# Row vectors written to DRAM four values at a time, and read back through strided views

## The chip, the cores and the metric

One core of a Trainium2 chip runs the whole program in one launch. The metric is the device time of one execution in microseconds (us). TensorE does the matrix products, VectorE (DVE in the profile) and GpSimd (POOL) the elementwise work, ScalarE (ACT) the activations and copies, and SyncE (SP) issues every DMA, strictly in the order of its queue.

## The reference

Two blocks run one after the other on one sequence of 512 tokens with 1024 features, in float32. The first block has two layers (a gated MLP mixer, then a sparse attention mixer, each followed by a squared-ReLU feed-forward of width 4096); the second is one layer of two attentions. Cut to what matters here:

```python
def modulate(h, shift, scale):
    return h * (1.0 + scale[:, None, :]) + shift[:, None, :]
...
    for layer in range(DEPTH):
        mod = c_act @ ada_w[layer] + ada_b[layer]
        sh1, sc1, g1, sh2, sc2, g2 = jnp.split(mod, 6, axis=-1)
        h = modulate(rms_norm(x, norm_g[layer, 0]), sh1, sc1)
        ...
        x = x + g1[:, None, :] * rms_norm(y, norm_g[layer, 1])
        h = modulate(rms_norm(x, norm_g[layer, 2]), sh2, sc2)
        y = jnp.square(jax.nn.relu(h @ ff_w_in[layer])) @ ff_w_out[layer]
        x = x + g2[:, None, :] * rms_norm(y, norm_g[layer, 3])
    return x
```

Each shift, scale and gate is a vector of 1024 values, one for each feature, and the same for all tokens. The second block ends with `x + gate * out` and has such a vector too.

## The kernel before

**Tiles.** Tokens are cut in four chunks of 128 (c0 to c3). The running sum `x` has its tokens on the partitions, one tile of 128x1024 for each chunk. The products take their operand with the features on the partitions, so at each boundary between two stages a chunk of `x` is normalised, scaled, shifted, transposed on TensorE and split in a high and a low half.

**Row vectors.** `vec` and `mod` compute a vector on VectorE (products of the transposed weights with the condition `cb`, 1 MB of weights at a time). It then lies on 128 partitions with 8 values in each: value 128k + p is in partition p, column k. `col` finishes it. Where the vector must multiply tiles with tokens on the partitions, it is needed as a row, the same on all partitions, and `wide` makes this: SP writes the 128x8 values to a scratch tensor of 1024 values in DRAM, and reads it back twice, each time 512 values copied to all 128 partitions. Eleven vectors go this way: G1, B2, S2 (end of the first mixer), G2 (end of the first feed-forward), G3, B4, S4 (end of the sparse attention), G5, B6, S6 (end of the second feed-forward), and the last gate. In the profile a copy has the vector's name with a w: G1w.

**Boundaries.** When a chunk's output product is done (its accumulator is `acc`, two banks of 512 columns), `residual` squares it on ScalarE, multiplies it by G on VectorE (`z<-acc,G1w`, two instructions of 512 columns), and adds it, scaled, to `x`. `x_rstd` makes the norm on ScalarE (`junkx`) with some small instructions. `h_chunk` multiplies by B (`hx<-x,B2w`, twice) and adds S (`hx<-hx,xr,S2w`, twice), then TensorE transposes (`tp<-ident,hx`). At the end of the first feed-forward `h_chunk2` does this with columns in place of rows, so that only the two products with G2 read a row there. In `fin`, the end of the program, the output is multiplied by the gate (`fy<-acc,gatew`), added to `x` and stored; the last 512 columns of c3 go in two halves.

**Order.** A planner (`Rec`) puts every instruction in a fixed order on each engine, by modelled costs and due times that come from the shapes. Each engine works in that order, and so does SP's DMA queue: a transfer that waits holds up all that stand behind it. In `out_gemm`, the products of the last `tail` weight rows run chunk after chunk, and the transposes of a chunk stand among the products of the next one, at the place where the planner expects their operand.

Of the kernel before, what the change touches and what calls it, by code (L numbers as in the profile page):

```python
# [672 lines left out]
class KB:  # L673
# [279 lines left out]
    def wide(self, vec, name):  # L953

        v = self.col(vec)
        r = self.scratch([1, 1024], name)
        self.sp.dma_start(r.rearrange("o (k p) -> p (o k)", p=128), v)
        t = [self.t2([128, 512], F32, name) for _ in range(2)]
        for n in range(2):
            self.sp.dma_start(t[n], r[:, n * 512:n * 512 + 512].bcast())  # L960
        return t


    def x_rstd(self, c, either=False):
# [32 lines left out]
    def h_chunk(self, c, r, B, S, hT, keep=None):  # L997
        if keep is not None:
            return self.h_chunk2(c, r, B, S, hT, keep)
        for n in range(2):  # L1000
            s = slice(n * 512, n * 512 + 512)
            t = self.t2([128, 512], F32, "hx")
            self.flex("tensor_mul", t, self.xs[c][:, s], B[n])
            self.mac(t, t, r, S[n])
            ps = self.ps("tp")
            for j in range(4):
                self.pe.transpose(ps[:, j * 128:(j + 1) * 128], t[:, j * 128:(j + 1) * 128], self.ident)
            cs = slice(c * 128, c * 128 + 128)
            self.split(hT.hi[n][:, :, cs], hT.lo[n][:, :, cs], ps.rearrange("p (j t) -> p j t", j=4))
# [17 lines left out]
    def residual(self, c, banks, G):  # L1027

        ss = self.st(2, "ys")
        z = []  # L1030
        for n in range(2):
            s = slice(n * 512, n * 512 + 512)
            junk = self.t2([128, 512], F32, "junk")
            self.act.activation(junk, banks[n], AF.Square, accum_out=ss[:, n:n + 1])
            z.append(self.t2([128, 512], F32, "z"))
            self.dve.tensor_mul(z[n], banks[n], G[n])
        r = self.rstd_of(ss, "yr")
        for n in range(2):
            s = slice(n * 512, n * 512 + 512)
            x = self.xs[c][:, s]  # L1040
            self.mac(x, z[n], r, x)
# [638 lines left out]
    def second(self, hT, grow):  # L1680
# [298 lines left out]
        gate = self.wide(grow, "gatew")  # L1979

        def fin(c, banks):
            for n in range(2):
                s = slice(n * 512, n * 512 + 512)
                xt = self.t2([128, 512], F32, "fx")
                self.sp.dma_start(xt, self.xd[c][:, s])
                y = self.t2([128, 512], F32, "fy")
                parts = 2 if c == NC - 1 and n == 1 else 1
                for i in range(parts):
                    h = slice(i * 512 // parts, (i + 1) * 512 // parts)
                    self.dve.tensor_mul(y[:, h], banks[n][:, h], gate[n][:, h])  # L1990
                    self.dve.tensor_add(y[:, h], y[:, h], xt[:, h])
                    self.sp.dma_start(self.out[0, c * 128:(c + 1) * 128, n * 512 + h.start:n * 512 + h.stop], y[:, h])

        self.out_gemm(self.act_f32(mixed), I["w_out_2"][0], KD, fin, CTAIL, split=True)

    def build(self):
# [87 lines left out]
```

## Time and profile before

| | |
|---|---|
| time before, median of 3 runs | 1547.93 us (1546.73 to 1547.94) |
| the profiled execution's own time | 1551.01 us |
| span of the profile | 1549.2 us |
| TensorE products busy | 1497.3 us, 97% |
| VectorE busy | 1084.5 us, 70% |
| ScalarE, GpSimd busy | 660.7 us, 284.8 us |
| chain that ended last, by engine | PE 83%, DVE 9%, DMA 3%, ACT 2%, issue 2%, POOL 1% |
| mean granted clock of TensorE | 0.989 |

The profile is one execution. Busy time is summed for each engine over the whole span; the chain that ended last is followed back from the last instruction, at each step to what it had waited for. All instructions that the planner emits have one line of the program (L616), so that the tiles' names tell them apart. Times in the trace count from the start of the span.

### The profile page before, as it was taken

The page shows a single profiled execution, that of the slowest core. Times are in us where ns is not written, and L with a number is a line of the kernel's source. Part 1 is how long each engine was busy: PE and PEld are TensorE (multiplying, and loading weights), DVE is VectorE, ACT ScalarE, POOL GpSimd, SP SyncE. Part 2 cuts the span into 40 slices and gives each one's busy share as a digit, 9 for nine tenths or more (in the row PEclk, how much of TensorE's full clock was granted, in tenths as well). Part 3 has the DMA queues.
Part 4 walks back from the last instruction along what each step waited for, and adds up shares of the span by engine and source line. Part 5 has one row for each costly group of instructions (what it writes and reads, how often), then busy time and mean ns, then how long its engine had stood idle before and what let it go on. Part 6 is the DMA issues. An engine that isn't in the chain of part 4 may idle for free.

```text
span 1549.2 us, 20191 instructions
## 1 busy us (share of the span) xinstructions
PE 1497.3 (97%) x7426; PEld 1253.7 (81%) x7426; DVE 1084.5 (70%) x2035; ACT 660.7 (43%) x1430; POOL 284.8 (18%) x349
## 2 busy tenths in 40 slices
PE   8995899999999999999998999999999999999998
PEld 6884688888888889788877898888888888878877
DVE  8895685557874378778898674556663568788992
ACT  6531342232121455577786332222120337667780
POOL 1122000000010130265655000000000004123250
PEclk9998899999999999999999999999999999999999
DMA  9872289447931071300015356538412161113212
GB/s 369 270 265 53 84 259 333 149 162 282 357 123 41 28 255 55 114 1 28 28 29 179 103 168 204 174 99 250 183 55 68 55 222 52 58 41 101 50 55 95
DMA packets 126370, 212.97 MB, mean 137 GB/s; under 512 B 24512, under 2 KB 85184, under 8 KB 126272
## 3 DMA queue, kind: packets, MB, share of 16 engines
q1 hardware_dynamic: 126272, 211.69, 41.0%
q8 instruction: 58, 0.95, 0.3%
q14 instruction: 40, 0.33, 0.1%
HBM read 205.33 MB, written 6.34 MB: 137 GB/s over the span
## 4 chain that ended last, share of the span: by engine, by line
PE 83%; DVE 9%; DMA 3%; ACT 2%; issue 2%; POOL 1%; POOLq 0%; SPq 0%; DVEq 0%; ACTq 0%
PE acc L616 28%; PE fmps L616 27%; PE vps L616 4%; PE qps L616 4%; PE tmc L616 4%; PE po L616 3%; DVE wl L616 2%; PE sgps L616 1%; PE tmb L616 1%; PE kps L616 1%; PE sB L616 1%; PE sA L616 1%; PE tp L616 1%; DVE ptl L616 1%; DMA G1w<-G 1%
## 5 line engine op out<-in xcount | busy, mean ns | idle before, releaser
L616 DVE TENSOR_TENSOR wl<-raw,wh 128x1024 fp32r<-128x1024 f32 x194 | 243.7, 1258 | 38.7 <-PE fmps L616 18.5
L616 PE MATMUL acc<-wl,ah 128*128 128x512 f32 x432 | 168.6, 390 | 0.0
L616 PE MATMUL acc<-wh,ah 128*128 128x512 f32 x432 | 168.4, 390 | 0.0
L616 DVE CAST wh<-raw 128x1024 fp32r<-128x1024 f32 x114 | 80.5, 706 | 120.6 <-PE fmps L616 94.4
L616 DVE SCALAR_TENSOR_TENSOR raw<-raw,cb 128x1024 f32<-128x1024 f32 x112 | 136.1, 1241 | 8.0 <-DMA raw<-in_kv_ada_w_dram 7.9
L616 PE MATMUL acc<-wh,al 128*128 128x512 f32 x432 | 133.6, 390 | 0.0
L616 ACT ACTIVATE r<-fmps 128x512 f32<-128x512 f32 x64 | 38.2, 597 | 205.9 <-PE fmps L616 205.9
L616 PE MATMUL acc<-twh,tah 128*128 128x512 f32 x272 | 106.9, 401 | 18.5 <-DVE twh L616 18.5
L616 PE MATMUL acc<-twl,tah 128*128 128x512 f32 x272 | 106.1, 399 | 0.5 <-DVE twl L616 0.5
L616 PE MATMUL fmps<-hfh,wl 128*128 128x512 f32 (+1 forms) x288 | 105.3, 367 | 0.7 <-DVE wl L616 0.7
L616 PE MATMUL fmps<-hf1l,wh 128*128 128x512 f32 (+1 forms) x288 | 105.4, 366 | 0.0
L616 PE MATMUL fmps<-hfl,wh 128*128 128x512 f32 (+1 forms) x288 | 105.4, 366 | 0.0
L616 PE MATMUL fmps<-hf1h,wl 128*128 128x512 f32 (+1 forms) x288 | 105.4, 366 | 0.0
L616 PE MATMUL fmps<-hfh,wh 128*128 128x512 f32 (+1 forms) x288 | 105.1, 366 | 0.0
L616 PE MATMUL fmps<-hf1h,wh 128*128 128x512 f32 (+1 forms) x288 | 105.0, 366 | 0.0
L616 ACT CAST ah<-hid 128x512 fp32r<-128x512 f32 x48 | 29.8, 620 | 158.9 <-PE acc L616 158.9
L616 PEld LDWEIGHTS acc<-wl,ah 128*128 128x128 f32 x432 | 81.2, 188 | 16.7
L616 PEld LDWEIGHTS acc<-wh,ah 128*128 128x128 f32 x432 | 81.1, 188 | 16.7
L616 PEld LDWEIGHTS acc<-wh,al 128*128 128x128 f32 x432 | 81.1, 188 | 16.7
L616 POOL TENSOR_SCALAR tah<-hid 128x512 fp32r<-128x512 f32 x4 | 4.2, 1038 | 471.6 <-DMA raw<-in_ff_w_out_dram 206.2
L616 PE MATMUL acc<-twh,tal 128*128 128x512 f32 x272 | 88.1, 398 | 0.6 <-DVE tal L616 0.6
L616 ACT CAST wh<-raw 128x1024 fp32r<-128x1024 f32 x59 | 61.8, 1050 | 50.5 <-PE fmps L616 35.5
(528 smaller groups left out, 3847.5 us busy)
## 6 DMA issues: line engine op xcount, KB each, us to landing
raw<-in_ada_w_dram SPq DMA_DIRECT2D x40, 1024.0 KB, 7.2
raw<-in_ff_w_in_dram SPq DMA_DIRECT2D x32, 1024.0 KB, 9.1
raw<-in_ff_w_out_dram SPq DMA_DIRECT2D x32, 1024.0 KB, 5.3
raw<-in_w_in_dram SPq DMA_DIRECT2D x16, 1024.0 KB, 5.5
raw<-in_w_ada_dram SPq DMA_DIRECT2D x12, 1024.0 KB, 11.5
raw<-in_ada_w_dram SPq DMA_DIRECT2D x16, 512.0 KB, 9.7
raw<-in_kv_ada_w_dram SPq DMA_DIRECT2D x8, 1024.0 KB, 14.3
raw<-in_a_w_in_dram SPq DMA_DIRECT2D x8, 512.0 KB, 10.2
```

Source lines behind the costliest of these rows:

```text
L616: getattr(real[e], m)(*a, **k)
```

## The change

`wide` writes the vector to DRAM in another order. In each half of 512 values, the four values that a partition has of this half now lie side by side: value 128k + p of a half goes to place 4p + k. What a partition writes is two runs of 4 values (16 bytes) in place of eight single values (4 bytes). The two reads that copy a half to all partitions are as before, so the copies have this order too, and `wide` gives out views of them with two free dimensions, k (step 1) and p (step 4), which run through the values in the old order. The instructions that read a row take these views; their other operands are viewed with the same two dimensions by `by4`, in which the values still lie side by side.

```diff
@@ wide
         v = self.col(vec)
         r = self.scratch([1, 1024], name)
-        self.sp.dma_start(r.rearrange("o (k p) -> p (o k)", p=128), v)
+        self.sp.dma_start(r.rearrange("o (n p k) -> p (o n) k", n=2, p=128), v.rearrange("p (n k) -> p n k", n=2))
         t = [self.t2([128, 512], F32, name) for _ in range(2)]
         for n in range(2):
             self.sp.dma_start(t[n], r[:, n * 512:n * 512 + 512].bcast())
-        return t
+        return [x.rearrange("q (p k) -> q k p", k=4) for x in t]
+
+    @staticmethod
+    def by4(x):
+
+        return x.rearrange("q (k p) -> q k p", k=4)
@@ h_chunk
-            self.flex("tensor_mul", t, self.xs[c][:, s], B[n])
-            self.mac(t, t, r, S[n])
+            self.flex("tensor_mul", self.by4(t), self.by4(self.xs[c][:, s]), B[n])
+            self.mac(self.by4(t), self.by4(t), r, S[n])
@@ residual
-            self.dve.tensor_mul(z[n], banks[n], G[n])
+            self.dve.tensor_mul(self.by4(z[n]), self.by4(banks[n]), G[n])
@@ fin
-                    self.dve.tensor_mul(y[:, h], banks[n][:, h], gate[n][:, h])
+                    hk = slice(h.start // 128, h.stop // 128)
+                    self.dve.tensor_mul(self.by4(y)[:, hk], self.by4(banks[n])[:, hk], gate[n][:, hk])
```

## Rows read from the trace of the kernel before

**Rows 1.** The chain of waits, 120 to 180 us: start, duration, what.
```profile
127.41 9.87 DMA B2w<-B
...
138.20 11.71 DMA G1w<-G
...
150.38 7.04 DMA raw<-in_a_w_out_dram
...
161.18 11.09 DMA S2w<-S
...
172.34 3.71 DMA S2w<-S2w
```
**Rows 2.** Timeline of PE, 118 to 210 us; in brackets its idle time before.
```profile
158.35 1.19 PE L616 MATMUL acc<-twh,tah 128*128 128x512 f32 x2 [18.46 <-DVE twh L616]
...
177.05 0.63 PE L616 MATMUL tp<-ident,hx 128*128 128x128 f32 x4 [1.97 <-DVE hx L616]
```
**Rows 3.** Windows: from:to, length, busy of PE to POOL, PEclk, DMA share, GB/s.
```profile
128.00:129.00 1.00, 0.96 (x4) 0.83 (x5) 1.00 (x1) 0.01 (x1) 0.00 (x0) 1.00 0.47 4
129.00:130.00 1.00, 1.00 (x7) 0.79 (x6) 1.00 (x4) 0.00 (x0) 0.00 (x0) 1.00 0.00 0
...
142.00:143.00 1.00, 0.00 (x0) 0.00 (x0) 0.00 (x0) 0.00 (x0) 0.00 (x0) 1.00 0.00 0
...
144.00:149.00 5.00, 0.00 (x0) 0.00 (x0) 0.00 (x0) 0.00 (x0) 0.00 (x0) 0.50 0.00 0
...
158.40:162.00 3.60, 3.60 (x9) 2.83 (x10) 2.75 (x4) 0.16 (x1) 0.00 (x0) 0.50 0.00 0
```
**Rows 4.** DMA issues of the run: size of one, median us to landing.
```profile
out_dram<-fy SPq DMA_DIRECT2D x2, 128.0 KB, 1.8
```
**Rows 5.** Groups of VectorE instructions by form: count, busy us, mean ns, idle before.
```profile
L616 DVE SCALAR_TENSOR_TENSOR bl<-R,pos,bh 128x124 fp32r<-128x124 f32 x32 | 13.2, 427 | 1.0 <-ACT bh L616 0.8
...
L616 DVE SCALAR_TENSOR_TENSOR mx<-pm,lngb,E 128x512 f32<-128x512 f32 x8 | 5.9, 744 | 1.5 <-PE pm L616 1.5
...
L616 DVE TENSOR_TENSOR z<-acc,G3w 128x512 f32<-128x512 f32 x8 | 5.2, 685 | 11.6 <-PE acc L616 11.6
...
L616 DVE SCALAR_TENSOR_TENSOR E<-wsum,lngb,bs 128x128 f32<-128x128 f32 x8 | 2.3, 336 | 0.0
```
**Rows 6.** Timeline of VectorE at the end of the first mixer, 164 to 178 us.
```profile
164.89 1.29 DVE L616 TENSOR_TENSOR z<-acc,G1w 128x512 f32<-128x512 f32 x2 [3.74 <-PE acc L616]
...
168.52 0.22 DVE L616 SCALAR_TENSOR_TENSOR rt<-yr,hv 128x1 f32<-128x1 f32 x1 [0.87 <-ACT yr L616]
...
176.15 1.41 DVE L616 SCALAR_TENSOR_TENSOR hx<-hx,xr,S2w 128x512 f32<-128x512 f32 x2 [3.19 <-DMA S2w<-S2w]
```
**Rows 7.** Timeline of VectorE at the end of the second feed-forward, chunk c0.
```profile
1208.60 1.29 DVE L616 TENSOR_TENSOR z<-acc,G5w 128x512 f32<-128x512 f32 x2 [31.22 <-PE acc L616]
...
1212.49 1.29 DVE L616 TENSOR_TENSOR hx<-x,B6w 128x512 f32<-128x512 f32 x2
1213.80 0.15 DVE L616 TENSOR_SCALAR hv<-ss 128x1 f32<-128x1 f32 x1
...
1214.90 1.42 DVE L616 SCALAR_TENSOR_TENSOR hx<-hx,xr,S6w 128x512 f32<-128x512 f32 x2
```
**Rows 8.** Timeline of PE there: the transposes of c0.
```profile
1216.56 0.60 PE L616 MATMUL tp<-ident,hx 128*128 128x128 f32 x4
```
**Rows 9.** Windows (columns as in rows 3): ends of the attention and the second feed-forward.
```profile
860.00:903.00 43.00, 43.00 (x252) 37.81 (x252) 36.68 (x77) 17.28 (x48) 1.67 (x1) 1.00 0.51 176
1208.00:1258.00 50.00, 50.00 (x238) 41.51 (x237) 36.90 (x84) 20.88 (x52) 3.26 (x4) 1.00 0.49 168
```
**Rows 10.** Timeline of VectorE and PE at the end of the first feed-forward, chunk c0.
```profile
522.72 0.48 DVE L616 TENSOR_SCALAR hx<-x,xr 128x512 f32<-128x512 f32 x1
...
524.15 1.03 PE L616 MATMUL tp<-ident,hx 128*128 128x128 f32 x8
```
**Rows 11.** Timeline of VectorE at the end of the program.
```profile
1545.02 0.76 DVE L616 TENSOR_TENSOR fy<-acc,gatew 128x256 f32<-128x256 f32 x2 [1.30 <-PE acc L616]
```

## The prediction

> **What bounds the kernel now.** I read the page first: TensorE is busy 97% of the span, so nearly every microsecond in which it stands still is on the path, and work on other engines counts only where TensorE waits for it. The chain of waits, in order of time, then shows where DMAs end last: the row vectors appear on it in one place only, the end of the first mixer [rows 1]. SP stands there behind the write of B2 (9.87 us), then behind that of G1 (11.71 us), and the load of the last rows of the mixer's output weights can only be issued after both, at 150.38. The timeline of PE shows what this costs: 18.46 us of standstill before 158.35 [rows 2]. S2's write (11.09 us) and its read back (3.71 us) are on the chain next; VectorE waits 3.19 us for them [rows 6] and TensorE 1.97 us [rows 2]. At the ends of the attention and of the second feed-forward TensorE is busy in all of the 43 and 50 us [rows 9], though VectorE makes every chunk's operand there.
>
> **What the write of a vector is made of.** In windows of 1 us, B2's write moves its packets between 128 and 129 (DMA share 0.47); from 129 on nothing moves, and yet it lands only at 137.28 [rows 1, 3]. So about 1.6 us pass to the last packet and 8.3 us after it, while 1024 single values settle in DRAM. I take the second part to go with the number of runs, 256 in place of 1024: 8.3/4 + 1.6 = 3.7 us. Bounds: 1.8 us, the landing of a store of 128 KB in long runs [rows 4], and no change. The nearer is the low one, since the settling is all of the difference to that store. G1's write shares the DMA engines with B2's two reads; its packets are through by 142 [rows 3], and of its 11.71 us the last 7.9 shrink to 2.0, leaving 5.8. S2's becomes 1.6 + 9.5/4 = 4.0 us.
>
> **What this gives at the first mixer's end.** G1's write is issued 0.92 us after B2's has landed, and the weight load 0.47 us after G1's [rows 1]. The load goes out at 127.41 + 3.7 + 0.92 + 5.8 + 0.47 = 138.3, 12.1 us earlier, and TensorE resumes at 158.35 - 12.1 = 146.3. It still stands for over 6 us. TensorE's clock fell to the lower of its two levels (granted 0.50) by 144, some 4 us into the standstill, and was still there after the restart [rows 3]; I assume that it falls again, so nothing is given back for it. With the 1.97 us wait gone, the transposes of c0 could run at 177.05 - 1.97 - 12.1 = 163.0. VectorE decides: its first product with G1 moves from 164.89 to 152.8; from there to the end of its first `hx<-hx,xr,S2w` (176.15 + 0.75) it took 12.0 us, of which the 3.19 for S2 go, because S2 is back at 161.18 - 12.1 + 4.0 + 3.7 = 156.8, before its turn. That would be 161.6 without dearer reads.
>
> **What a strided read costs.** 89 instructions read a row with step 4: 32 with G, 24 with B (one on GpSimd), 24 with S, 9 with the gate. The trace has no such step, but one neighbour: `bl<-R,pos,bh` reads one of its inputs with a step of 16 values and takes 427 ns for 124 columns [rows 5]. The same operation without the step takes 336 ns for 128 columns (E) and 744 for 512 (mx), which makes 1.06 ns a column and 200 ns fixed, so 332 ns for 124. The step costs 95 ns in 124 columns, 0.77 ns each, and 0.40 us in 512. The view in three dimensions alone costs nothing: mx has one too, and lies on the line of its kind. Bounds for 512 columns: nothing (a step of four values is nearer to contiguous than one of 16), and 0.54 us, a second pass over the 512 columns at 1.06 ns. I take 0.40, from the row. [...]
>
> **Where it falls on the path.** In c0 of the first mixer, seven such instructions come before the first transposes (four z, two of them c1's, two B, one S): 2.8 us, of which some 0.6 disappear in a wait for ScalarE (0.87) [rows 6]. c0's transposes then run at 161.6 + 2.8 - 0.6 + 0.1 = 163.9, against 177.05: **13.1 us gained**. From c1 to c3 VectorE is nearly saturated and the transposes stand in TensorE's queue just behind their operand; six instructions add 2.4 us a chunk, less some 0.4 of slack: 3 x 2.0 = **6.0 us lost** (c3 has one fewer on VectorE, but no slack).
>
> The other ends have the same pattern with nothing to win. At the end of the second feed-forward c0's chain runs z (two), x, B (two), small instructions, S (two). `hv` follows B with no gap [rows 7], so all six are in line. The first S ends at 1215.65, the transposes begin at 1216.56 [rows 7, 8]: 0.9 us of slack, 0.75 after the hand-over. TensorE takes the transposes in order, among c1's products, so it stands 2.4 - 0.75 = 1.65 us, the next chunk's accumulator is late by as much, and the same happens again. There are four chunks here and four at the end of the attention: 8 x 1.65 = **13.2 us lost**. At the end of the first feed-forward only the two z are slower, 0.8 us against about 0.9 of slack between the normalised chunk and its transposes [rows 10]: nothing, and what is over 0.75 if the step is dearer. At the end of the program two products of 256 columns stand in a row before the last store [rows 11]: **0.4 us**. The write costs of the other eight vectors lie under products of TensorE and give nothing back. The planner's costs come from shapes that don't change, so I expect the same order.
>
> **Sum.** 13.1 - 6.0 - 13.2 - 0.4 = -6.5: slower by 6.5 us. The profiled execution took 1551.01 us, 3.08 above the median of the runs; 1557.5 for it, and 1547.93 + 6.5 = 1554.4, so 1554 us, for the median. With the step at 0.30 or 0.50 us and all else alike, the sum runs from 1 us faster to 13 slower: 1547 to 1561 is this case's own range.
>
> **Rivals.**
> *The strided reads are (nearly) free.* Place: the eight chunks above. Below some 0.12 us an instruction the slack of 0.75 swallows them, and only the first mixer's gain is left. For it: no row has a step as short as four values. Against: the row with 16. At no cost TensorE sets c0's transposes at 163.0, 14 us gained: 1534 us; at 0.2 us, 1540. The point where it turns is near 0.3. [...]
> *A strided column takes a whole second pass* (0.54 us). For it: the row lies at three quarters of that. 12.1 - 8.5 - 8 x 2.49 - 0.5 = -17: 1565 us, and the queues fill further beyond. [...]
> *The write does not get shorter.* Then nothing is gained at the first mixer, its c0 hides its dearer reads in the 3.19 us wait, and 6.0 + 13.2 + 0.4 make 1567 us. For it: the DMA engines are idle for most of the write, so the packets' number is not what they work on. Against: the settling is absent for long runs [rows 4].
> *The clock stays up*, because the write lands in 2 us and the standstill ends before 144. TensorE's products up to c0's end then run at the full level, which is worth at most half of the 6.5 us from 158.35 to 164.89; I take 2.6, with 2 more from the writes: 1550 us, and 1546 with the step at 0.35 us.
>
> **Chances.** The forecast 0.54; free reads 0.18; second pass 0.13; write unchanged 0.07; clock up 0.08. A measurement here can tell some 0.2% (3.1 us) from no change. Faster by more: nearly all of the free reads, half of the clock case and a little of the first, 0.22. Within: a third of the forecast and most of the rest of the clock case, 0.20. Slower: 0.58. For 8 in 10 the range takes in the unchanged write and half of the two stride rivals: 1538 to 1570.
>
> **What would show it.** In the profile after: writes of vectors landing in 3 to 6 us, SP issuing the weight load near 138, TensorE's standstill at 6 us; `z`, `hx` and `fy` with rows at 1.05 to 1.15 us in place of 0.68 to 0.75; short waits of TensorE for `hx` in each of the eight chunks of rows 9's stretches, 1 to 2 us each. The forecast is wrong if those instructions keep their time, if TensorE stays busy in those stretches in spite of them, or if the writes still take 10 us.

## The result, and the profile after

| | before | after |
|---|---|---|
| median of the runs on one chip | 1547.93 us (1546.73 to 1548.36) | 1558.3 us (1554.39 to 1559.49) |
| ratio, with its 95% interval | | 1.0057 [1.0041, 1.0072] |
| the profiled execution's own time | 1551.01 us | 1554.39 us |
| span of the profile, mean granted clock | 1549.2 us, 0.989 | 1552.6 us, 0.993 |
| TensorE, VectorE busy | 1497.3, 1084.5 us | 1501.0, 1117.3 us |
| DMA packets, of them under 512 bytes | 126370, 24512 | 117922, 16064 |
| chain that ended last | PE 83%, DVE 9%, DMA 3% | PE 77%, DVE 15%, DMA 1% |

The change makes the kernel slower, by 10.4 us in the medians and by 3.4 us in the two profiles (why these differ is taken up with the last experiment). Every engine runs the same instructions on the same tiles in the same order as before, so the traces can be compared row by row. The chain already points the way: DMA's share of it falls from 3 to 1%, and VectorE's rises from 9 to 15%.

The gain is where it was expected, at the end of the first mixer. The chain of waits there, in the columns of [rows 1]:

```profile
127.36 2.56 DMA B2w<-B
...
130.85 3.19 DMA G1w<-G
...
134.50 7.44 DMA raw<-in_a_w_out_dram
```

The two writes take little over a quarter of their time [rows 1], and the weight load goes out 15.9 us earlier. The timeline of PE:

```profile
142.88 0.70 PE L616 MATMUL acc<-twh,tah 128*128 128x512 f32 x2 [2.99 <-DVE twh L616]
...
159.34 0.63 PE L616 MATMUL tp<-ident,hx 128*128 128x128 f32 x4 [0.73 <-DVE hx L616]
...
168.15 0.63 PE L616 MATMUL tp<-ident,hx 128*128 128x128 f32 x4 [1.66 <-DVE hx L616]
```

The standstill is 2.99 us in place of 18.46, and c0's transposes come 17.7 us earlier [rows 2]; but TensorE now waits for `hx` in all four chunks: 0.73 and 1.66 us in the lines above, 1.22 us in c2 (at 178.11) and 2.06 us in c3 (192.44), where before it waited 1.97 us in c0 and 1.05 us in c3. Of the other writes, four in the list of DMA issues (size, us to landing; before, these four took 11.1, 11.0, 9.9 and 9.7 us):

```profile
S2w<-S SPq DMA_DIRECT2D x1, 4.0 KB, 1.6
...
G2w<-G SPq DMA_DIRECT2D x1, 4.0 KB, 2.9
...
G3w<-G SPq DMA_DIRECT2D x1, 4.0 KB, 1.7
...
G5w<-G SPq DMA_DIRECT2D x1, 4.0 KB, 3.0
```

The slowest of the rest are S4's, 16.8 us before and 2.7 after, and S6's, 13.5 and 6.1.

What takes the gain back stands in the groups of VectorE by form, here two of before,

```profile
L616 DVE SCALAR_TENSOR_TENSOR hx<-hx,xr,S6w 128x512 f32<-128x512 f32 x8 | 5.7, 748 | 0.1
...
L616 DVE TENSOR_TENSOR hx<-x,B6w 128x512 f32<-128x512 f32 x8 | 5.1, 686 | 0.0
```

and four of after:

```profile
L616 DVE SCALAR_TENSOR_TENSOR bl<-R,pos,bh 128x124 fp32r<-128x124 f32 x32 | 13.2, 426 | 1.0 <-ACT bh L616 0.8
...
L616 DVE SCALAR_TENSOR_TENSOR hx<-hx,xr,S6w 128x512 f32<-128x512 f32 x8 | 8.7, 1131 | 0.1
...
L616 DVE TENSOR_TENSOR hx<-x,B6w 128x512 f32<-128x512 f32 x8 | 8.3, 1082 | 0.0
L616 DVE TENSOR_TENSOR z<-acc,G3w 128x512 f32<-128x512 f32 x8 | 8.3, 1067 | 11.0 <-PE acc L616 11.0
```

The `z` with G3 took 685 ns [rows 5] and now takes 1067; the `hx` with B6 and with S6 took 686 and 748 ns and now take 1082 and 1131. That is 0.38 to 0.40 us for 512 columns, or 0.75 to 0.77 ns a column. With B2, B4 and the gate it is 0.37 to 0.41 us, with S4 0.49 in the mean, where one pair of instructions took 2.96 us (at 881.32) and the others 2.18 to 2.24. `bl`, which the change doesn't touch, is as it was. The windows that answer to [rows 9], and two of the low clock (columns as in [rows 3]):

```profile
144.00:148.00 4.00, 3.93 (x11) 2.77 (x10) 1.68 (x3) 0.00 (x0) 0.00 (x0) 0.58 0.04 1
...
860.00:903.00 43.00, 37.83 (x231) 33.27 (x231) 41.49 (x67) 14.86 (x39) 1.98 (x1) 0.96 0.64 217
884.00:888.00 4.00, 3.58 (x17) 3.51 (x18) 4.00 (x7) 1.60 (x5) 0.00 (x0) 0.58 1.08 381
1208.00:1258.00 50.00, 44.67 (x207) 35.55 (x206) 41.48 (x71) 17.57 (x43) 2.85 (x4) 1.00 0.51 169
```

TensorE, which filled both stretches [rows 9], now stands for 5.17 of 43 and 5.33 of 50 us. In the first of them the waits for `hx` over 0.3 us are 0.95, 1.35, 1.31 and 0.97 us (c0, c1 and the two halves of c2; c3 has none). In the second stretch the timeline of PE names who was late, in each of the four chunks:

```profile
1213.94 0.63 PE L616 MATMUL tp<-ident,hx 128*128 128x128 f32 x4 [0.88 <-DVE hx L616]
...
1227.21 0.63 PE L616 MATMUL tp<-ident,hx 128*128 128x128 f32 x4 [0.91 <-DVE hx L616]
...
1242.21 0.63 PE L616 MATMUL tp<-ident,hx 128*128 128x128 f32 x4 [1.74 <-DVE hx L616]
...
1256.70 0.63 PE L616 MATMUL tp<-ident,hx 128*128 128x128 f32 x4 [1.00 <-DVE hx L616]
```

**A table by stage.** SP issues the write of a vector at a fixed place in the kernel's order, so these writes cut the span in five stretches. In the timeline of SP, first before, then after:

```profile
223.30 0.37 SPq L616 DMA_DIRECT2D G2w<-G  x1
...
795.77 0.38 SPq L616 DMA_DIRECT2D G3w<-G  x1
...
925.27 0.37 SPq L616 DMA_DIRECT2D G5w<-G  x1
...
1453.05 0.37 SPq L616 DMA_DIRECT2D gatew<-gate  x1
```

```profile
209.65 0.37 SPq L616 DMA_DIRECT2D G2w<-G  x1
...
782.58 0.38 SPq L616 DMA_DIRECT2D G3w<-G  x1
...
921.61 0.37 SPq L616 DMA_DIRECT2D G5w<-G  x1
...
1456.07 0.37 SPq L616 DMA_DIRECT2D gatew<-gate  x1
```

The first stretch holds the end of the first mixer, the third the end of the attention, the fourth that of the second feed-forward. So the first stretch became 13.7 us shorter, the second 0.5 longer, the third 9.5, the fourth 6.7 and the last 0.4. The experiments are read by these stretches.

### The profile page after: what moved, and what is told of

The parts are those of the page before. It is cut to its first block, busy times and chain, and to the rows that moved or that the text cites. A ratio compares the mean times of both kernels' runs of the same rounds, so it can differ in the third digit from the quotient of the medians.

```text
span 1552.6 us, 20198 instructions
## 1 busy us (share of the span) xinstructions
PE 1501.0 (97%) x7426; PEld 1252.3 (81%) x7426; DVE 1117.3 (72%) x2035; ACT 661.9 (43%) x1430; POOL 285.4 (18%) x349
## 2 busy tenths in 40 slices
DMA packets 117922, 212.97 MB, mean 137 GB/s; under 512 B 16064, under 2 KB 76736, under 8 KB 117824
## 4 chain that ended last, share of the span: by engine, by line
PE 77%; DVE 15%; ACT 3%; issue 3%; POOL 1%; DMA 1%; POOLq 0%; SPq 0%; DVEq 0%; ACTq 0%
PE fmps L616 26%; PE acc L616 24%; PE qps L616 4%; PE tmc L616 4%; PE vps L616 3%; PE po L616 3%; DVE hx L616 3%; DVE wl L616 2%; PE sgps L616 1%; DVE z L616 1%; PE sB L616 1%; PE kps L616 1%; PE sA L616 1%; DVE x L616 1%; DVE ptl L616 1%
## 5 line engine op out<-in xcount | busy, mean ns | idle before, releaser
L616 PEld LDWEIGHTS acc<-wh,al 128*128 128x128 f32 x432 | 81.4, 188 | 16.8
L616 PEld LDWEIGHTS acc<-wl,ah 128*128 128x128 f32 x432 | 81.4, 188 | 16.8
```

Of the source, the lines that this page charges most:

```text
L616: getattr(real[e], m)(*a, **k)
```

## The experiments

Theory: the runs of 16 bytes give the gain, all of it at the first mixer's end, and the strided reads take it back at three boundaries, because `hx` comes later than the slack of its transposes. Rivals: the gain comes from less DMA traffic altogether, or the loss from something else than the step (the order, the planner, TensorE's clock).

**The changed kernel once more (e0_again).** No edit.

> The changed kernel itself once more, to see what its executions have in common: the profile taken first lost 3.4 us of span against the one of before, the median of the runs 10.4. Theory A (the strided reads cost TensorE short waits at two boundaries, and the clock it is granted around them differs from execution to execution): median 1555 to 1560 again, and executions whose mean granted clock is lower are longer. Rival B (a fixed time cost that the profile hid): all executions within 0.1% of one time, whatever their clock.

Measured: 1558.5 us (1552.63 to 1561.27, 6 runs) against 1549.0 (11 runs), ratio 1.0051 [1.0034, 1.0069]. The profile of this one has a span of 1559.5 us, 6.9 more than the first with the same instructions. Its windows show where:

```profile
620.00:632.00 12.00, 10.38 (x41) 8.05 (x42) 9.78 (x12) 3.73 (x5) 0.00 (x0) 0.72 0.48 157
...
888.00:892.00 4.00, 4.00 (x23) 3.90 (x21) 4.00 (x8) 1.18 (x3) 0.00 (x0) 0.57 1.06 384
...
1516.00:1520.00 4.00, 3.98 (x12) 3.27 (x13) 2.93 (x4) 1.31 (x2) 0.00 (x0) 0.57 0.20 66
```

The clock was low in stretches in which the first profile has it at full level (1.00 from 620 to 632 and from 1516 to 1520). Theory A holds: the shortest of the six runs (1552.6 us) has the highest mean granted clock, 0.992, the one at 0.990 took 1557.2, and the four at 0.986 or 0.987 took 1558.5 to 1561.3. So two profiles of one kernel can differ by 7 us, twice what the first two profiles give for the change.

**The write alone (e1_write).** The reads are contiguous, so the copies have their values in DRAM's order, which is not the order that the products need. Against the kernel before:

```diff
-        self.sp.dma_start(r.rearrange("o (k p) -> p (o k)", p=128), v)
+        self.sp.dma_start(r.rearrange("o (n p k) -> p (o n) k", n=2, p=128), v.rearrange("p (n k) -> p n k", n=2))
```

> The new write alone: the vector goes to DRAM four values side by side, and the rows are read contiguously as before, so that the products take the vector's values in another order than they belong. Theory A: the gain at the first mixer's end (13.7 us in the profile, with dearer reads in it) shows in full and some more, nothing else moves: 1548 - 16 = 1532 us, within 3. Rival C (VectorE sets the first mixer's end anyway, the shorter write gives little): 1541 to 1548.

Measured: 1530.3 us (1529.21 to 1533.05), ratio 0.9881 [0.9864, 0.9897]. The whole gain lies ahead of the write of G2, which is issued at 202.4 (before 223.3); the other stretches are within 1 us of before. The chain of waits shows a first mixer without dear reads:

```profile
142.31 15.49 PE acc L616 x60
157.79 0.44 PE tp L616 x4
```

TensorE's products run straight into c0's transposes, and up to there nobody waits for VectorE.

**The strided reads alone (e2_read).** The write stays in single values, so that here too the products take a vector's values in another order than they belong. Against the changed kernel:

```diff
-        self.sp.dma_start(r.rearrange("o (n p k) -> p (o n) k", n=2, p=128), v.rearrange("p (n k) -> p n k", n=2))
+        self.sp.dma_start(r.rearrange("o (k p) -> p (o k)", p=128), v)
```

> The strided reads alone: the write is the old one in single values, the rows are read through views with step 4, so that the products take the vector's values in another order than they belong. Theory A: z, hx and fy instructions at 1.06 to 1.13 us as in the changed kernel, the losses of 9.5 us at the attention's end and 6.7 at the second feed-forward's, 0.4 at the end, and 4 to 6 at the first mixer's: 1548 + 22 = 1570 us, within 4. Rival D (the losses come from the earlier clock pattern and not from the reads): under 1558.

Measured: 1574.3 us (1572.46 to 1575.5), ratio 1.0161 [1.0145, 1.0178], 0.3 us above theory A's range; by its stretches 5.8 us lost in the first, 0.6 in the second, 8.0 in the third, 6.7 in the fourth and 0.4 in the last. The two parts alone give -18.7 and +25.3 us, together +6.6, where the whole change measures +9.5.

**The change at the first mixer alone (e3_first).** G1, B2 and S2 go the new way, the other eight the old one.

```diff
+        four = name in ("G1w", "B2w", "S2w")
...
-        return t
+        return [x.rearrange("q (p k) -> q k p", k=4) for x in t] if four else t
```

> The change for the three vectors of the first mixer's end alone (G1, B2, S2), written four side by side and read strided; the other eight as before. Theory A: keeps the 13.7 us, loses nothing later: 1534 us, within 3. Rival B (a cost outside the two later boundaries): 1540 or more.

Measured: 1539.3 us (1536.57 to 1540.8), ratio 0.9933 [0.9919, 0.9948]: 9.8 us faster, 4 less than I expected; that is 2 us above theory A's range and 0.7 below rival B's 1540. G2's write is issued at 210.5, as in the whole change (209.65) and 8.1 us after that of the write alone (202.4). So the strided reads cost 8 us at this boundary too (some 1.6 of them are a low clock from 194 to 198 that the write alone doesn't have, by the estimate explained with the last experiment), and the rest of the loss lies at the two later ends: its third and fourth stretch are 130.5 and 527.9 us, within 1 us of before.

**Two instructions a chunk dearer, or four (e5_z, e7_bs).** As e3_first, with the new way also for G3 and G5 (two `z` a chunk, 0.8 us), or for B4, S4, B6 and S6 (four `hx`, 1.6 us).

```diff
-        four = name in ("G1w", "B2w", "S2w")
+        four = name in ("G1w", "B2w", "S2w", "G3w", "G5w")
...
-        four = name in ("G1w", "B2w", "S2w")
+        four = name in ("G1w", "B2w", "S2w", "B4w", "S4w", "B6w", "S6w")
```

> As the kernel with the change for G1, B2 and S2 alone (1539.25 us), and with the change for G3 and G5 too; B4, S4, B6 and S6 stay as before the change. At the ends of the attention and of the second feed-forward only the two z of a chunk are then dearer, 0.8 us a chunk. Theory A (the prediction's slack: 0.75 us between a chunk's operand and its transposes swallow the first part): the two stretches from the write of G3 to that of G5 and from there to the gate's stay at 129.5 to 130.8 and 527.8 to 528.5 us, and the run stays within 1 us of that kernel, 1539 to 1541 us. Rival B (VectorE is the bound in these stretches and every dearer instruction counts in full): a third of the whole loss, 2.5 to 3.2 us more in the first stretch and 2 in the second, 1544 us.

> As the kernel with the change for G1, B2 and S2 alone (1539.25 us), and with the change for B4, S4, B6 and S6 too; G3 and G5 stay as before the change. Four instructions a chunk are dearer by 0.4 us each, 1.6 us. Theory A (slack of 0.75 us a chunk): 0.85 us a chunk, 3.4 us in each of the two stretches, 1546 us. Rival B (every dearer instruction counts in full): two thirds of the loss of all six, 5 to 6.4 us in the first stretch and 4.5 in the second, 1549 to 1550 us.

Measured: 1541.9 us (1538.9 to 1543.43), ratio 0.9951 [0.9939, 0.9963], and 1549.0 us (1544.19 to 1550.27), 0.9997 [0.9989, 1.0006]; that is 2.8 and 9.9 us more than e3_first by the ratios. The end of the second feed-forward in windows of 50 us, first e5_z:

```profile
1197.20:1247.20 50.00, 49.40 (x233) 40.39 (x232) 39.68 (x81) 20.04 (x51) 4.02 (x4) 1.00 0.49 169
```

and e7_bs:

```profile
1199.40:1249.40 50.00, 47.67 (x218) 38.04 (x217) 40.28 (x72) 18.78 (x48) 3.63 (x4) 1.00 0.46 153
```

TensorE stands 0.60 us with two dearer instructions a chunk, 2.33 with four, 5.33 with all six: not in proportion, but from a slack on. The fourth stretch is 529.4 and 532.4 us, but each of these profiles has a low clock well behind the feed-forward's end (1350 to 1356 and 1356 to 1362), which takes 1.5 and 1.6 us (an estimate, explained with the last experiment). With that out they are 0.1 and 2.9 us above e3_first, and the whole change is 6.6; theory A has 0.2 and 3.4 here, and the prediction 6.6. At the attention's end the third stretch is 131.9 and 134.7 us against 130.5. With a low clock of 3.2, 3.4 and 2.4 us taken out by the same estimate, that is 0.7 and 3.2 us more; in the 43 us that answer to [rows 9] (852.9 to 895.9 and 855.1 to 898.1) TensorE stands for 1.48 and 3.02 us (0.96 of the 1.48 in one wait for a `wl`), for none in e3_first and 5.17 with all six. By the time of the whole run the answer is split: e5_z lies 1 us above A's range and 2 below B's number, e7_bs at B's. So a slack as in theory A is shown at both ends once the low clock is out, and it is not enough to give the whole run.

**No step at all (e4_natural).** The rows of the weights are loaded so that a partition holds four neighbouring values from the start; the write has runs of 16 bytes, the copies come back in natural order.

Against the kernel before (`row` is false for four vectors that `wide` doesn't write):

```diff
-            self.sp.dma_start(raw, W[col0 + 128 * j:col0 + 128 * j + 256].rearrange("(j p) n -> p j n", p=128))
+            if row:
+                k = j % 4
+                w = W[col0 + j // 4 * 512:col0 + j // 4 * 512 + 512].rearrange("(p k) n -> p k n", k=4)
+                self.sp.dma_start(raw, w[:, k:k + 2])
+            else:
+                self.sp.dma_start(raw, W[col0 + 128 * j:col0 + 128 * j + 256].rearrange("(j p) n -> p j n", p=128))
...
-        self.sp.dma_start(r.rearrange("o (k p) -> p (o k)", p=128), v)
+        self.sp.dma_start(r.rearrange("o (n p k) -> p (o n) k", n=2, p=128), v.rearrange("p (n k) -> p n k", n=2))
```

The small vectors that `col` adds and multiplies are laid out in the new order where the inputs are prepared, as they were in the old order before.

> The rows of the weights are loaded so that partition p holds the values 4p to 4p+3 of each half from the start; the writes are in runs of 16 bytes, the copies come back in natural order, and no view has a step. The time of the write alone was 1530.3 us (0.988 of before). Theory A (the write's runs give the gain, the step of the reads takes it back; how the weights are loaded costs nothing, since a partition still reads whole rows of 4 KB, two in a row instead of two far apart): 1530 us, 1527 to 1534. Theory B (the gain of the write alone came from anything else in that kernel, or the new loads of the weights are slower and delay the vectors): 1540 us or more.

Measured: 1529.6 us (1529.05 to 1533.62), ratio 0.9883 [0.9868, 0.9899]: by the ratio 18 us faster than before, and by the medians 29 faster than the change. The loads of weights in the new order take no longer (7.1 us in the median for 1 MB of `ada_w`, 7.2 before). At the end of the second feed-forward TensorE is full again:

```profile
1185.80:1235.80 50.00, 50.00 (x237) 41.51 (x236) 36.89 (x84) 20.93 (x52) 3.16 (x4) 1.00 0.49 165
```

**A planner that knows the price (e6_told).** The whole change, and the planner's cost of an instruction that reads a row grows by 0.77 ns a column.

```diff
     def cost(self, e, m, a, k):
+        return self.cost0(e, m, a, k) + 0.77 * (a[0].cells()[1] if m != "dma_start" and any(
+            isinstance(x, V) and id(x.buf) in STEP for x in a) else 0)
...
+        STEP.update(id(x.buf) for x in t)
```

> The whole change, and the planner is told that an instruction which reads a row with step 4 takes 0.77 ns a column longer, so that it orders all engines anew. Theory A (the loss at the ends comes from transposes that stand too early in TensorE's order; with later places TensorE does other products meanwhile): half or more of the 16 us at the two ends comes back, 1545 to 1552 us. Rival B (VectorE's own throughput, 41.5 us busy in 43 and 50, is the bound, so that no order helps): 1555 to 1560 us, as the change itself.

Measured: 1552.1 us (1549.54 to 1560.63, 12 runs), ratio 1.0024 [1.0012, 1.0036], some 4 us better than the change by the ratios (6 by the medians) and still slower than before; it lies at the upper end of theory A and 3 us below rival B. At the end of the second feed-forward, from 1195 to 1265 the timeline of PE has one wait over 0.3 us, and it is not for `hx`:

```profile
1247.28 0.50 PE L623 MATMUL tmb<-wl,h2h 128*128 128x512 f32 x1 [1.33 <-DVE wl L623]
```

So later places for the transposes hide most of the loss there. At the attention's end they don't: there TensorE still stands for 4.54 of 43 us, 3.85 of them in one wait for VectorE, before the transposes at 888.89.

```profile
860.00:903.00 43.00, 38.46 (x240) 34.35 (x239) 40.40 (x63) 17.28 (x40) 6.68 (x4) 0.92 0.65 220
```

And the new order issues the weight load at the first mixer's end at 138.69 in place of 134.50 and gives G2's write at 213.3, 3.7 us later than the change: a part of the gain is paid for elsewhere. So theory A is shown at one of the two ends only.

**Which steps cost, and how much (e8_steps).** Products of VectorE on 512 columns, added behind the end of e4_natural:

```diff
+        for k in (2, 4, 8, 16, 64):
+            t = self.t2([128, 512], F32, f"ml{k}")
+            for _ in range(4):
+                self.dve.tensor_mul(nat(t, k), nat(self.last, k), hop(g, k))
```

where `hop` views a tile with step k and `nat` gives the other operands the same two dimensions. (The run's own time, 1562.8 us, has the added products in it and says nothing here.)

> The kernel that loads the weights in the new order (1529.6 us), with 44 products of VectorE added behind the end of the program, whose results nobody reads: four each of tensor_mul on 512 columns with one source read with a step of 1, 2, 4, 8, 16 and 64 values, with only the target written with a step of 4, with both sources read with a step of 4, and on runs of 1, 2 and 3 values out of each 4 (128, 256, 384 columns, all three operands alike). Theory A (every column that does not lie next to the one before costs the same; the 16-value row and the change's 4-value step agree): about 0.68 us at step 1 and 1.05 to 1.08 us at 2, 4, 8, 16 and 64. Rival B (the cost grows with the step, and 4 only happens to lie near 16): step 2 well below 4, 64 well above 16. Where both sources hop: a second surcharge of 0.38 us (1.45 us), or, if the two reads hop at the same time, none (1.07 us). Runs of 2: no surcharge (0.44 us for 256 columns) if a run of two adjacent values streams at full rate, else 0.62 us.

The timeline of VectorE, one source with a step of 2, 4, 8, 16 and 64 values, in this order:

```profile
1530.43 0.69 DVE L616 TENSOR_TENSOR ml<-ml,gatew 128x512 f32<-128x512 f32 x1
1531.04 1.05 DVE L616 TENSOR_TENSOR ml<-ml,gatew 128x512 f32<-128x512 f32 x1
1532.02 1.07 DVE L616 TENSOR_TENSOR ml<-ml,gatew 128x512 f32<-128x512 f32 x1
1533.00 1.01 DVE L616 TENSOR_TENSOR ml<-ml,gatew 128x512 f32<-128x512 f32 x1
1533.93 1.02 DVE L616 TENSOR_TENSOR ml<-ml,gatew 128x512 f32<-128x512 f32 x1
```

and the groups by form: target with step 4 (`md`), both sources with step 4 (`mb`), no step (`ml<-fy`), runs of 3, 2 and 1 out of each four values (`mr`), and a contiguous product of the kernel's own with 256 columns (`fy<-fy,fx`):

```profile
L616 DVE TENSOR_TENSOR md<-ml,gatew 128x512 f32<-128x512 f32 x4 | 4.2, 1061 | 0.0
L616 DVE TENSOR_TENSOR mb<-ml,gatew 128x512 f32<-128x512 f32 x4 | 4.2, 1040 | 0.0
...
L616 DVE TENSOR_TENSOR ml<-fy,gatew 128x512 f32<-128x512 f32 x4 | 2.8, 692 | 0.1
...
L616 DVE TENSOR_TENSOR mr<-ml,gatew 128x384 f32<-128x384 f32 x4 | 2.2, 554 | 0.0
...
L616 DVE TENSOR_TENSOR mr<-ml,gatew 128x256 f32<-128x256 f32 x4 | 1.7, 421 | 0.0
...
L616 DVE TENSOR_TENSOR mr<-ml,gatew 128x128 f32<-128x128 f32 x4 | 1.5, 379 | 0.0
...
L616 DVE TENSOR_TENSOR fy<-fy,fx 128x256 f32<-128x256 f32 x2 | 0.8, 416 | 0.0
```

A step of 2 costs nothing (0.69 us, as without a step), steps from 4 to 64 cost the same 0.32 to 0.38 us, a hopping target as much as a hopping source, and two hopping sources no more than one. Theory A is right from 4 up and wrong at 2; rival B is right at 2 and wrong from 4 up. From 692 ns at 512 and 416 at 256 contiguous columns a column costs 1.08 ns, which makes 554 ns for 384 columns and 278 for 128. The runs of 3 and 2 lie within 5 ns of this line (554 and 421); the single values out of four take 379, 0.79 ns a column more.

**Other lengths of run in the write (e9_runs).** As the write alone, with runs of 2 values for G1, G2, G3 and G5 and of 8 for the rest.

```diff
+        runs = 4 if name[0] in "G" else 1
+        k = 8 // runs
-        self.sp.dma_start(r.rearrange("o (n p k) -> p (o n) k", n=2, p=128), v.rearrange("p (n k) -> p n k", n=2))
+        self.sp.dma_start(r.rearrange("o (n p k) -> p (o n) k", n=runs, p=128), v.rearrange("p (n k) -> p n k", n=runs))
```

> The write alone, with contiguous reads and so with the values of a row in another order, but in runs of 2 values (8 bytes, 512 runs) for G1, G2, G3 and G5 and of 8 values (32 bytes, 128 runs) for the others. Landing of the write of G1, G2, G3, G5: with runs of 1 value 11.7, 11.0, 9.9, 9.7 us, of 4 values 3.2, 2.9, 1.7, 3.0. Theory A (the time goes with the number of runs): halfway down by count, 4.5 to 6 us for these four; B2 and the others with 128 runs 2 us. Rival B (only single values settle slowly): 2 to 3.5 us for runs of 2, as for runs of 4, and the whole run at 1530 us. With A the run takes some 2 us more, 1532 to 1533 us.

The list of DMA issues:

```profile
B2w<-B SPq DMA_DIRECT2D x1, 4.0 KB, 1.4
G1w<-G SPq DMA_DIRECT2D x1, 4.0 KB, 5.0
...
G2w<-G SPq DMA_DIRECT2D x1, 4.0 KB, 4.1
...
G3w<-G SPq DMA_DIRECT2D x1, 4.0 KB, 3.1
...
G5w<-G SPq DMA_DIRECT2D x1, 4.0 KB, 4.8
```

For G1, G2, G3 and G5: 256 runs 3.2, 2.9, 1.7 and 3.0 us, 512 runs 5.0, 4.1, 3.1 and 4.8, 1024 runs 11.7, 11.0, 9.9 and 9.7. With runs of 8 values (128 runs) B2, S2, B6 and the gate took 1.4 us each, B4 and S4 2.8, S6 4.7. So the time grows with the number of runs, but not in proportion: the second 256 runs add 1.2 to 1.8 us, the next 512 add 4.9 to 6.9. The truth lies between the theories: with 512 runs G1 and G5 are in A's 4.5 to 6 us, G3 is in B's 2 to 3.5, and G2 is between. The single run took 1532.1 us, where A said 1532 to 1533 and B 1530; one run doesn't tell these apart.

**Before and after profiled again (e10_before, e11_after).** No edit.

> The kernel before, profiled once more. The medians say that the change costs 8 to 10 us, the first two profiles 3.4 us. Theory A (executions of one kernel differ by where TensorE's clock falls and by nothing else; the changed kernel loses more that way than its first profile shows): with the time lost to a low clock taken out (PE's busy time times one minus the granted clock, over windows of 2 us), the stretches between the writes of G2, G3, G5 and the gate are as in the first profile of before, within 1 us, 572.5, 126.3, 527.8 and 96.1 us, and the clock takes some 10 us in all, as there (9.7). Rival B (executions also differ in DMA landings or waits): a stretch that is off by over 2 us without a low clock in it.

> The changed kernel, profiled a third time; its first two profiles have spans of 1552.6 and 1559.5 us. Theory A: with the time lost to a low clock taken out, the stretches are 206 to 207 us to the write of G2, 573, 132 to 133, 534 and 96.4 us, and what the clock takes is nearer to 15 us than to the 9.8 us of its first profile, in stretches of 4 to 12 us at places that differ from profile to profile. Rival B: a stretch that is off by over 2 us without a low clock in it.

Measured: spans of 1542.5 and 1553.5 us (1544.2 and 1555.2 us with what lies around). What a low clock takes is an estimate from the rows: the sum, over windows of 2 us, of PE's busy time times one minus the granted clock. By stretches, in us, "of it clock" being this estimate (the profiles come from more than one chip, so a difference between chips would be in these numbers too):

| stretch | before, 2 profiles | of it clock | after, 3 profiles | of it clock | difference of the means | without the clock |
|---|---|---|---|---|---|---|
| to G2's write | 223.3, 219.7 | 6.5, 6.2 | 209.7, 211.8, 210.3 | 3.4, 5.1, 4.6 | -10.9 | -8.9 |
| to G3's | 572.5, 572.3 | 0, 0 | 572.9, 576.0, 573.0 | 0, 3.1, 0 | +1.6 | +0.5 |
| to G5's | 129.5, 126.5 | 3.2, 0 | 139.0, 137.1, 139.1 | 6.4, 5.0, 6.2 | +10.4 | +6.1 |
| to the gate's | 527.8, 527.8 | 0, 0 | 534.5, 536.6, 534.5 | 0, 3.3, 0 | +7.4 | +6.3 |
| to the end | 96.1, 96.2 | 0, 0 | 96.5, 98.0, 96.6 | 0, 1.7, 0 | +0.9 | +0.3 |
| sum | | 9.7, 6.2 | | 9.8, 18.2, 10.8 | +9.3 | +4.3 |

From the second stretch on, the executions of one kernel agree within 1.2 us once the clock is out: theory A holds there. The first stretch of before is 216.8 and 213.5 us without the clock, 3.3 apart, more than A allows. The trace tells where 1.2 us of it come from: from the issue of B2's write to that of the weight load, with TensorE at full level or standing, it took 22.97 us in the first profile [rows 1] and 21.82 in the second, above all because G1's write landed sooner there (before in 11.71 us, here in 9.36):

```profile
138.51 9.36 DMA G1w<-G
```

That part is rival B's. Nearly all of the rest lies ahead of B2's write, where both profiles have low clock; whether the estimate is off there stays open. The clock took 6.2 us in the second profile of before where A said some 10, and 10.8 in the third of after where A said nearer to 15: both misses.

## Why the prediction was right, and where its sizes were off

The direction and the place of every part held: 1554 us was forecast and 1558.3 measured, slower as forecast. The sum of 6.5 us was 4 us short. That it came so near is in part luck: without the low clock its own terms come to 4.3 us, and the 5.0 us on top are clock, which the sum had at nothing.

*The writes* were mis-sized. The step "I take the second part to go with the number of runs" gave 3.7, 5.8 and 4.0 us; they took 2.56, 3.19 and 1.6. The run lengths show that the part is not in proportion: going from 256 to 512 runs adds 1.2 to 1.8 us, from 512 to 1024 4.9 to 6.9. Why the second step is dearer stays open, and so does what happens between a write's last packet and its landing: that values settle there was the author's reading, and the trace shows the time alone (8.3 us for B2). So the weight load went out at 134.50 (predicted 138.3), TensorE resumed at 142.88 (146.3), and c0's transposes came at 159.34 (163.9): 17.7 us gained in place of 13.1.

*The clock at the restart* fell as assumed (a mean of 0.58 from 144 to 148), but was back by 148, where before it was low until 162 at least [rows 3]. The rival "the clock stays up" was half true; by the table some 2 us of the gain in the first stretch are the clock's.

*The price of the step* was right: 0.40 us predicted from `bl` with its step of 16 values, 0.38 to 0.40 measured in most groups of the kernel. The steps from 4 to 64 show that the neighbour was a good one. No run shows the 0.35 us that the rival of the clock also reckons with; they showed the 0.38 to 0.40 in the kernel, and 0.32 to 0.38 in the products added for the steps. The rival of free reads would have been right for a step of two values (0.69 us, as without a step). Adjacent values alone don't decide it: runs of two and three were free here (421 and 554 ns for 256 and 384 columns), but so was the step of 2, in which no two values are adjacent.

*The loss from c1 to c3* of the first mixer was 17.7 - 13.7 = 4.0 us against the first profile of before, predicted 6.0; but that profile has a low clock from 178 to 182 (1.7 us by the estimate), which the change's doesn't have. The write alone is the better measure, with as much low clock in this stretch as the changed kernel (3.3 and 3.4 us): against it c0's transposes come 1.55 us later (159.34 and 157.79) and G2's write 7.3 (209.65 and 202.35), so c1 to c3 lose 5.8.

*The ends of the attention and the second feed-forward* were predicted to lose 13.2 us; without the clock they lost 6.1 + 6.3 = 12.4, of which 5.17 + 5.33 = 10.5 are standstill. The 1.65 us a chunk were counted with one instruction too many: by [rows 7] and [rows 8] only the first of the two S stands ahead of the first transposes, so five dearer instructions do and not six, 5 x 0.385 - 0.75 = 1.2 us, and the second half waits some 0.2 more (at 1215.00). For four chunks that gives 5.5 us with all six, 2.5 with B and S alone and nothing with z alone; measured were 5.33, 2.33 and 0.60. So the slack of 0.75 us is right within some 0.15 us a chunk.

*The end of the program* cost 0.3 (predicted 0.4), *the first feed-forward's end* 0.5 (predicted nothing).

*What the sum left out* is the clock in the later stretches. With the clock out, the table gives +4.3 us; with it, +9.3, near the difference of the medians (9.5 and 10.4). The biggest part, 4.3 us, lies in the third stretch. Of it 1.6 us lie between 884 and 892, where all three profiles of after have a low clock (0.50 from 884.5 to 888 in the first), just behind the four waits for `hx` or among them, and no profile of before has one. That the waits bring it about is not shown. The other 2.7 us lie between 802 and 838, ahead of the first dearer instruction of that end (852.07): after has two stretches of low clock there in each profile (0.50 from 802.75 to 809.5 and from 830 to 833.5 in the first), before one and none (0.50 from 816.25 to 823.25), and kernels with contiguous reads one or two (e4_natural 0.79 from 796 to 804; e9_runs 0.50 from 796 to 802 and from 824 to 826); the changed reads can't be shown to bring these about either. Nor is it shown why the changed kernel drops in some executions at 620 or 1516, far from any row.

That the loss could be hidden is shown in part: the order made with the true price lost little at the second feed-forward's end, but still stood for 4.54 us at the attention's, and gave up 3.7 us at the first mixer. That none of it need be paid is shown by the natural order: with the same runs of 16 bytes and no step it takes 1529.6 us.

## What to carry to other kernels

Count the runs of a small store, not its bytes: 4 KB in 1024 single values mostly took 10 to 12 us to land (S4 and S6 16.8 and 13.5) and in 256 runs of four 1.6 to 3.5 (S6 6.1), and where a queue works in order that is paid by everything behind it (the weight load behind two such writes went out at 150.38, and at 134.50 when they were short). Get the new layout from the side where it is free (here the order in which weight rows are loaded, 7.1 us for 1 MB against 7.2), not from a strided read in an instruction that runs once for every tile. Before a view with a step is put into an operand, find the engine's slack at that very place: VectorE was busy 72% of the span, and 0.38 to 0.40 us more in six instructions a chunk still stopped TensorE.

## What the runs showed of the hardware that was not expected

- VectorE reads one source with a step of 2 values as fast as without a step (0.69 us for 512 columns), and steps of 4, 8, 16 and 64 cost the same (1.01 to 1.07 us). A hopping target costs as much (1.06), and two hopping sources together no more than one (1.04).
- The landing of a 4 KB write is not in proportion to its number of runs, and the step from 512 to 1024 costs most: G1 took 3.2 us with 256 runs, 5.0 with 512 and 11.7 with 1024; B2 took 1.4 with 128, 2.6 with 256 and 9.9 with 1024.
- Executions of the same instructions differ by up to 7 us in span (1552.6 and 1559.5), and with what the low clock takes by the estimate left out, by 1.2 us or less in each of the five stretches of the changed kernel. The first stretch of the kernel before differs by 3.3, 1.2 of them because a write landed sooner.
